# First layer's experts: one written order on TensorE, token transposes around half of the down products, one down tile split

## The chip, the cores and the metric

The kernel runs on one core of one Trainium2 chip. The metric is device time in microseconds of that core, the median of several runs; less is better. Beside the timed runs one execution was recorded by the hardware profiler, and every trace row below comes from that execution.

## The reference, cut to what matters

The program is a two-layer transformer for 1024 latent tokens and 256 context tokens, of width 1024. Each layer ends with 16 experts. An expert takes the 128 latent tokens (and, in the first layer alone, also the 32 context tokens) that score best for it:

```
xg  = h[idx]                                     # 128 x 1024, chosen rows
hid = silu(xg @ w_gate) * (xg @ w_up)            # 128 x 512
out = (hid @ w_down) * vals                      # 128 x 1024
y   = zeros.at[idx].add(out)                     # added back to the tokens
```

The weights of one expert are six tiles of 1 MB: two of `w_gate`, two of `w_up`, two of `w_down`, all in fp32. In the second layer the context tokens are no longer needed (`need` is false there).

## The kernel before, in words

**Products.** `expert_up` computes the gate and up products of the latent tokens as three products of rounded fp32r operands: a weight tile `est` is split by `split` into a high part (`ewh`, a cast on ScalarE, L1178) and a low part (`ewl`, a subtraction on VectorE that reads `est` and `ewh`, L1182), and the tokens into `xh` and `xo`; the products are `xh*wh`, `xo*wh`, `xh*wl` (L1280). The split tiles live in three buffers each. The down products of the latent tokens (`pd`, L1335) are plain fp32 products on the unsplit tile; each is recorded as two passes of TensorE. The context tokens are only 32 rows, so their products run with `tile_position`, four at a time, each in 32 columns of the array: gate and up as `pgc` (L1265), two folding steps as `hcp` (L1309), down as `pdc` (L1341). I call such products quarter products.

**Tokens.** `expert_x` turns the gathered rows: four transposes into PSUM bank 4 (`xt`, L1231), a multiplication on VectorE (`xm`, L1233), an addition on GpSimd (L1234), a cast on ScalarE (`xh`, L1235), a subtraction on VectorE (`xo`, L1236), and the same again for the second four; then two transposes `xtc` for the context tokens, with `xct` on VectorE. `expert_hid` makes `hid`, transposes it through the same bank 4 (`hidp`, L1300) and copies it to `hidT`; it also folds the context part (`hcp`), computes `hidc` and transposes it (`hct`, L1317). `slots` (L1148) finds the tokens of a later expert with ten tiny products `slp`.

**Order.** The program is written as a loop over 16 experts: slots and loads of expert e+3, `expert_hid(e)`, `expert_x(e+2)`, `expert_up(e+1)`, `expert_down(e)`. That is not the order on the engines: a planner runs the program once in its own timing model and places every instruction on its engine's queue when the model finds it ready. On the chip each queue then runs in exactly that order, and waits for data by semaphores. `issue_after` tells the planner to place an instruction behind another.

**Loads.** SyncE issues the weight loads into a ring of nine `est` buffers, in the order gate and up of expert e, then down of expert e-1. GpSimd issues the gathers (`xg`, `xgc`) and the scatters that add an expert's result to the tokens in DRAM (`yo`, `yc`, L1170).

**Banks.** PSUM has eight banks. Gate and up of the latent tokens use banks 0 and 1, down 2 and 3, `xt` and `hidp` share bank 4, `pgc` has bank 5, and `hcp`, `hct` and `pdc` share bank 6.

Of the kernel before, what the change touches and what calls it, by code (L numbers as in the profile page):

```python
# [19 lines left out]
P = 128  # L20
# [22 lines left out]
class Kern:  # L43
# [1177 lines left out]
    def expert_x(self, l, r, ep, eng=None):  # L1221
# [6 lines left out]
        for k in range(0, KD, 4):  # L1228
            ps = self.bank("xt" if need else "xt2", [P, 4, P], F32, "xt")
            for j in range(4):  # L1230
                nc.tensor.transpose(ps[:, j], xg[:, (k + j) * P:(k + j + 1) * P], self.idf)  # L1231
            xm = ep.tile([P, 4, P], F32, name="xm", bufs=2)
            nc.vector.tensor_tensor(xm, ps, self.A2[:, 0, k:k + 4].unsqueeze(2).to_broadcast([P, 4, P]), ALU.mult)  # L1233
            (eng or nc.gpsimd).tensor_tensor(xm, xm, mt[:, 0, 24 + k:28 + k].unsqueeze(2).to_broadcast([P, 4, P]), ALU.add)  # L1234
            nc.scalar.copy(xh[:, k:k + 4], xm)  # L1235
            r["xd"] = nc.vector.tensor_tensor(xo[:, k:k + 4], xm, xh[:, k:k + 4], ALU.subtract)  # L1236
        r["x"] = (xh, xo)
        if need:
# [4 lines left out]
            for c in range(2):  # L1243
                nc.tensor.transpose(ps[:, c], xgc[:, c * P:(c + 1) * P], self.idf)
# [5 lines left out]

    def expert_up(self, l, r, ep, first=False):
# [4 lines left out]
        pc, sc = None, []  # L1256

        def ctx_mm(gu, hf, st):

            nonlocal pc  # L1260
            if hf == 0:
                pc = self.bank("upc", [P, 512], F32, "pgc")
            for k in range(4):
                kk = 4 * hf + k
                nc.tensor.matmul(pc[32 * k:32 * k + 32], r["xc"][:, kk % 2, 32 * (kk // 2):32 * (kk // 2) + 32],  # L1265
                                 st[:, 512 * k:512 * k + 512], start=hf == 0, stop=hf == 1, tile_position=(0, 32 * k),
                                 skip_group_check=True)
            if hf == 1:
                t = ep.tile([P, 512], F32, name=f"sc{gu}", bufs=1)
                nc.scalar.copy(t, pc)  # L1270
                sc.append(t)
        late = []
        for gu in range(2):
            n = 0
            for hf in range(2):
                st = r[("gate", "up")[gu]][hf]
                wh, wl = r["pre"].pop(0) if r.get("pre") else self.split(self.ws, st, [P, 2048], "ew", 3)
# [5 lines left out]
                if need:  # L1283
                    late.append((gu, hf, st))
                    if len(late) > 1 * first:
                        ctx_mm(*late.pop(0))
        for x in late:
            ctx_mm(*x)
        return acc, sc

    def expert_hid(self, l, r, up, ep):
        nc = self.nc
        need = l < DEPTH - 1
        (pg, pu), sc = up
        hid = ep.tile([P, 512], F32, name="hid", bufs=1 + need)
        nc.scalar.activation(hid, pg, AF.Silu)
        nc.vector.tensor_tensor(hid, hid, pu, ALU.mult)
        ps = self.bank("xt" if need else "downc", [P, 4, P], F32, "hidp")
        for j in range(4):
            nc.tensor.transpose(ps[:, j], hid[:, j * P:(j + 1) * P], self.idf)  # L1300
        hT = ep.tile([P, 4, P], F32, name="hidT", bufs=2)
        nc.scalar.copy(hT, ps)  # L1302
        if need:

            ps = self.bank("downc", [P, 256], F32, "hcp")
# [5 lines left out]
            hc, uc = [ep.tile([64, 256], F32, name=n, bufs=1) for n in ("hidc", "upc")]  # L1311
            nc.scalar.activation(hc, ps[:64], AF.Silu)
            nc.vector.tensor_copy(uc, ps[64:])
            nc.vector.tensor_tensor(hc, hc, uc, ALU.mult)
            ps = self.bank("downc", [P, 2, 64], F32, "hct")
            for c in range(2):
                nc.tensor.transpose(ps[:, c], hc[:, P * c:P * c + P], self.idf[:64, :64])  # L1317
            hcT = ep.tile([P, 2, 2, 32], F32, name="hcT", bufs=2)
            nc.vector.tensor_copy(hcT.rearrange("p h c s -> p c h s"), ps.rearrange("p c (h s) -> p c h s", h=2))
        return hT, (hcT if need else None)  # L1320

    def expert_down(self, l, r, hid, ep, g5, g5c, xl, xc):
# [3 lines left out]
        if need:  # L1326
            pd = self.bank("downc", [P, 512], F32, "pdc")
        po = [self.bank("down", [P, 512], F32, "pd") for _ in range(2)]
        for hf in range(2):
            st = r["down"][hf]  # L1330

            for k in range(2):
                for nn in range(2):
                    c = 1024 * k + 512 * nn
                    self.downed = nc.tensor.matmul(po[nn], hT[:, 2 * hf + k], st[:, c:c + 512],  # L1335
                                                   start=hf == 0 and k == 0, stop=hf == 1 and k == 1)
            for k in range(2):
                if need:
                    for nn in range(2):
                        o = 64 * k + 32 * nn  # L1340
                        nc.tensor.matmul(pd[o:o + 32], hcT[:, hf, k], st[:, 1024 * k + 512 * nn:1024 * k + 512 * nn + 512],  # L1341
# [197 lines left out]
```

## Time and profile before

| what | us |
|---|---|
| median of 3 timed runs | 2732.65 (2731.37 to 2734.65) |
| the profiled execution's own time | 2732.13 |
| its span, first to last instruction | 2730.4 |
| experts of the first layer, first gate product to last down product | 1005.7 to 1447.3 |

The span is 1.7 us below the execution's own time; a change inside the span is added to the 2732.13. The experts of the first layer repeat with one period per expert, so that a change there is read from one period and multiplied. A period can be taken between any two equal events of neighbouring experts; here it is the start of the gate's `silu` on ScalarE.

### The profile page before, as it was taken

To read this page: it belongs to the slowest core of one execution; us is meant where nothing else is said; L and a number is where in the kernel's file an instruction comes from. 1 tells how busy PE (TensorE), PEld (TensorE's weight loads), DVE (VectorE), ACT (ScalarE), POOL (GpSimd) and SP (SyncE) were. 2 spreads that over 40 slices of the span, in tenths; PEclk is the share of its full clock that TensorE was granted. 3 is DMA by queue.
4 is the path that set the end of the run, shared out by engine and by line. 5 is a ranking of instruction groups with operands and counts; after the bars stand their busy time and mean duration, and the time that the engine had idled before them with its cause. 6 is when DMAs were issued, how large, how long until landed. Compare 5 with 4: busy or idle time off the path is not lost.

```text
span 2730.4 us, 55190 instructions
## 1 busy us (share of the span) xinstructions
PE 2504.4 (92%) x21959; PEld 1906.9 (70%) x21959; DVE 1884.3 (69%) x4046; ACT 1131.4 (41%) x1878; POOL 669.3 (25%) x621
## 2 busy tenths in 40 slices
PE   7999999998999979999996999999958899589997
PEld 4998887894677855555554988778844677367664
DVE  4258887857666586777754368787858874787874
ACT  4224433324554534444434334333314554345452
POOL 1000000035444633333311000000045532222241
PEclk9999999998999979999998999999979999789999
DMA  7332324247354948888887332423176355889994
GB/s 281 102 108 71 114 68 123 66 138 243 113 160 135 349 151 278 281 280 279 283 280 212 94 105 74 124 84 89 49 200 225 94 163 183 300 281 370 377 376 127
DMA packets 347936, 507.12 MB, mean 186 GB/s; under 512 B 53380, under 2 KB 203072, under 8 KB 346592
## 3 DMA queue, kind: packets, MB, share of 16 engines
q1 hardware_dynamic: 336416, 465.85, 50.4%
q0 software_dynamic: 11264, 37.75, 5.9%
q8 instruction: 173, 2.83, 0.4%
q14 instruction: 83, 0.68, 0.1%
HBM read 410.10 MB, written 94.90 MB: 185 GB/s over the span
## 4 chain that ended last, share of the span: by engine, by line
PE 67%; DVE 18%; DMA 5%; issue 4%; ACT 3%; POOL 2%; SPq 1%; POOLq 0%; DVEq 0%; ACTq 0%
PE pg L1280 13%; PE pj L277 12%; PE pd L1335 8%; PE pj L288 8%; PE po L828 6%; PE nao L786 3%; PE pgc L1265 2%; PE npt L762 2%; PE sA L733 1%; DVE Kt L375 1%; PE aps L157 1%; DVE Kt L376 1%; DVE Qt L378 1%; PE hl L365 1%; PE xt L1231 1%
## 5 line engine op out<-in xcount | busy, mean ns | idle before, releaser
L1182 DVE TENSOR_TENSOR ewl<-est,ewh 128x2048 fp32r<-128x2048 f32 x126 | 298.1, 2371 | 109.7 <-ACT ewh L1178 108.6
L1178 ACT CAST ewh<-est 128x2048 fp32r<-128x2048 f32 x128 | 243.4, 1905 | 170.9 <-PE pg L1280 130.5
L277 PE MATMUL pj<-hl,whi 128*128 128x320 f32 (+2 forms) x912 | 310.2, 340 | 0.0
L277 PE MATMUL pj<-hh,whi 128*128 128x320 f32 (+2 forms) x912 | 309.9, 340 | 0.0
L277 PE MATMUL pj<-hh,wlo 128*128 128x320 f32 (+2 forms) x912 | 308.7, 339 | 0.0
L288 PE MATMUL pj<-whi,hh 128*128 128x256 f32 x960 | 277.8, 290 | 4.5 <-ACT nev L566 4.1
L288 PE MATMUL pj<-whi,hl 128*128 128x256 f32 x960 | 276.8, 291 | 0.8 <-DVE hl L239 0.8
L288 PE MATMUL pj<-wlo,hh 128*128 128x256 f32 x960 | 275.5, 288 | 0.0
L1335 PE MATMUL pd<-est,hidT 128*128 128x512 f32 x512 | 232.2, 596 | 2.1 <-ACT hidT L1302 2.1
L288 PEld LDWEIGHTS pj<-whi,hh 128*128 128x128 f32 x960 | 186.0, 194 | 8.8 <-ACT nev L566 5.2
L288 PEld LDWEIGHTS pj<-wlo,hh 128*128 128x128 f32 x960 | 185.9, 194 | 2.2 <-issue 1.3
L288 PEld LDWEIGHTS pj<-whi,hl 128*128 128x128 f32 x960 | 184.6, 194 | 3.5 <-issue 1.3
L277 PEld LDWEIGHTS pj<-hh,whi 128*128 128x128 f32 x912 | 172.2, 189 | 13.7 <-issue 0.9
L277 PEld LDWEIGHTS pj<-hl,whi 128*128 128x128 f32 x912 | 172.2, 189 | 13.5 <-issue 1.9
L277 PEld LDWEIGHTS pj<-hh,wlo 128*128 128x128 f32 x912 | 172.1, 189 | 13.0 <-issue 1.1
L1335 PEld LDWEIGHTS pd<-est,hidT 128*128 128x128 f32 x512 | 95.2, 189 | 110.7 <-issue 103.3
L265 DVE TENSOR_TENSOR wlo<-wst,whi 128x1024 fp32r<-128x1024 f32 (+1 forms) x72 | 75.2, 1058 | 131.7 <-ACT whi L264 130.6
L1280 PE MATMUL pg<-ewh,xh 128*128 128x512 f32 x512 | 156.8, 424 | 3.1 <-ACT xh L1235 3.0
L752 POOL TENSOR_SCALAR S<-S,sm 128x768 f32<-128x768 f32 (+2 forms) x108 | 108.6, 1007 | 188.3 <-DVE sm L751 166.8
L1280 PE MATMUL pg<-ewl,xh 128*128 128x512 f32 x512 | 147.7, 404 | 0.0
L1280 PE MATMUL pg<-ewh,xo 128*128 128x512 f32 x512 | 142.3, 398 | 2.1 <-DVE xo L1236 2.1
L750 ACT ACTIVATE S<-S,mn 128x768 f32<-128x768 f32 (+2 forms) x108 | 98.6, 913 | 85.2 <-DVE mn L745 79.6
(369 smaller groups left out, 5560.9 us busy)
## 6 DMA issues: line engine op xcount, KB each, us to landing
est<-in_w_exp_gate_dram SPq DMA_DIRECT2D x64, 1024.0 KB
est<-in_w_exp_up_dram SPq DMA_DIRECT2D x64, 1024.0 KB
est<-in_w_exp_down_dram SPq DMA_DIRECT2D x64, 1024.0 KB
wm<-in_w_mod_dram SPq DMA_DIRECT2D x80, 512.0 KB
wst<-in_w_in_dram SPq DMA_DIRECT2D x88, 256.0 KB
pna<-nev SPq DMA_DIRECT2D x180, 64.0 KB
wos<-in_w_out_dram SPq DMA_DIRECT2D x42, 256.0 KB
mst<-mix SPq DMA_DIRECT2D x32, 320.0 KB
```

Of the source, the lines that this page charges most:

```text
L265: nc.vector.tensor_tensor(b, c, a, ALU.subtract)
L277: nc.tensor.matmul(ps[:, :cn], sel(a(k)), b[:, k, c0:c0 + cn], start=n == 0, stop=n == 3 * KD - 1)
L288: nc.tensor.matmul(ps[:, :2 * P], b[:, k, t * P:(t + 1) * P], a(k).rearrange("p a n -> p (a n)"), start=n == 0, stop=n == 3 * KD - 1)
L750: nc.scalar.activation(S[:, :w], S[:, :w], AF.Exp, scale=-1.0, bias=mn[:, 1:2], accum_out=sm[:, 0:1])
L752: nc.gpsimd.tensor_scalar(S[:, :w], S[:, :w], sm[:, 1:2], 1.0, ALU.mult, ALU.mult)
L762: nc.tensor.transpose(pt[:kn, i], S[:, c:c + kn], self.idf)
L786: nc.tensor.matmul(po[64 * X:64 * X + 64, gi], V[:kn, tt, 64 * X:64 * X + 64], PT[X][:kn, i], start=i == 0, stop=i == len(ch) - 1, tile_po ...
L828: nc.tensor.matmul(ps, a, b, start=n == 0, stop=n == len(ops) - 1)
L1178: nc.scalar.copy(hi, src)
L1182: nc.vector.tensor_tensor(lo[:, :m], src[:, :m], hi[:, :m], ALU.subtract)
L1280: nc.tensor.matmul(acc[gu], a[:, 4 * hf + k], b[:, 512 * k:512 * k + 512], start=n == 0, stop=n == 3 * KD - 1)
L1335: self.downed = nc.tensor.matmul(po[nn], hT[:, 2 * hf + k], st[:, c:c + 512], start=hf == 0 and k == 0, stop=hf == 1 and k == 1)
```

## The change

Only the first layer's experts change in what is computed where (the second layer takes the same functions with `need` false; there `hid` of an expert is written behind the down products of the one before, instead of ahead of the next loads).

1. A helper `then` chains every matmul and transpose issued under it behind the one before. TensorE's order becomes the program's: gate products of e+1, all 32 quarter products of gate and up, up products, the fold `hcp`, then the quarter products of down of e, four token transposes of e+2, the first half of down, four more transposes and `xtc`, the second half of down, `hidp` and `hct` of e+1. Only `slp` stays free.
2. The quarter products are no longer interleaved with the split products: `pgc` of gate and up follow each other, in banks 5 and 6, and `hcp`, `hct` move to bank 5.
3. The second of the two down tiles is split (`ewh`, `ewl`), and so is half of `hidT` (`hTh`, `hTl`); that half of down becomes twelve fp32r products instead of four fp32 products (eight passes).
4. `hidc` and its transposes span 128 partitions instead of 64.

```diff
+    def expert_xs(self, l, r, ep, eng=None, order=False):
...
             for j in range(4):
-                nc.tensor.transpose(ps[:, j], xg[:, (k + j) * P:(k + j + 1) * P], self.idf)
+                with self.then(order):
+                    nc.tensor.transpose(ps[:, j], xg[:, (k + j) * P:(k + j + 1) * P], self.idf)
...
+            if k == 0:
+                yield
...
+    @contextmanager
+    def then(self, on=True):
+        nc, tc = self.nc, self.tc
...
+        def after(f):
+            def g(*a, **k):
+                with tc.issue_after(self.pel.ins) if self.pel is not None else nullcontext():
+                    self.pel = f(*a, **k)
+                return self.pel
+            return g
+        nc.tensor.matmul, nc.tensor.transpose = after(mm), after(tr)
...
+        def ctx_mm(gu):
+            pc = self.bank(("upc", "downc")[gu], [P, 512], F32, "pgc")
+            for hf in range(2):
...
+        with self.then(need):
+            prods(0)
+            if need and not first:
+                ctx_mm(0)
+                ctx_mm(1)
+            prods(1)
+            if need and first:
+                ctx_mm(0)
+                ctx_mm(1)
...
+    def expert_ctx(self, sc):
+        ps = self.bank("upc", [P, 256], F32, "hcp")
+        with self.then():
...
+    def expert_ctx_hid(self, ps, ep):
+        hc, uc = ep.tile([P, 256], F32, name="hidc", bufs=1), ep.tile([64, 256], F32, name="upc", bufs=1)
+        nc.scalar.activation(hc, ps, AF.Silu)
+        nc.vector.tensor_copy(uc, ps[64:])
+        nc.vector.tensor_tensor(hc[:64], hc[:64], uc, ALU.mult)
+        pt = self.bank("upc", [P, 2, P], F32, "hct")
+        with self.then():
             for c in range(2):
-                nc.tensor.transpose(ps[:, c], hc[:, P * c:P * c + P], self.idf[:64, :64])
+                nc.tensor.transpose(pt[:, c], hc[:, P * c:P * c + P], self.idf)
...
+            hh, hl = [ep.tile([P, 2, P], F32R, name=n, bufs=2) for n in ("hTh", "hTl")]
+            nc.scalar.copy(hh, hT[:, 2:])
+            nc.vector.tensor_tensor(hl, hT[:, 2:], hh, ALU.subtract)
+            self.hTs = (hh, hl)
...
+    def expert_down(self, l, r, hid, ep, g5, g5c, xl, xc, mid=None):
         if need:
+            hTh, hTl = self.hTs
+            wh, wl = self.split(self.ws, r["down"][1], [P, 2048], "ew", 3)
             pd = self.bank("downc", [P, 512], F32, "pdc")
+            with self.then():
...
+            next(mid, None)
         po = [self.bank("down", [P, 512], F32, "pd") for _ in range(2)]
         for hf in range(2):
+            if hf == 1:
+                next(mid, None)
+            with self.then(need):
...
+                        if need and hf == 1:
+                            for i, (a, b) in enumerate(((hTh, wh), (hTl, wh), (hTh, wl))):
+                                self.downed = nc.tensor.matmul(po[nn], a[:, k], b[:, c:c + 512], start=False,
+                                                               stop=k == 1 and i == 2)
+                            continue
...
             for e in range(NE):
                 if e + 3 <= NE:
                     start(e + 3, rs[e + 1]["xd"])
-                hid = self.expert_hid(l, rs[e], up, ep)
-                if e + 2 < NE:
+                if not need and e + 2 < NE:
                     self.expert_x(l, rs[e + 2], self.xp)
                 if e + 1 < NE:
                     up = self.expert_up(l, rs[e + 1], ep)
-                self.expert_down(l, rs[e], hid, ep, g5, g5c, xl, xc)
+                    if need:
+                        pc = self.expert_ctx(up[1])
+                more = iter(())
+                if need and e + 2 < NE:
+                    more = self.expert_xs(l, rs[e + 2], self.xp, order=True)
+                self.expert_down(l, rs[e], (hid, hidc if need else None), ep, g5, g5c, xl, xc, more)
+                if e + 1 < NE:
+                    hid = self.expert_hid(l, rs[e + 1], up, ep)
+                    if need:
+                        hidc = self.expert_ctx_hid(pc, ep)
```

## Rows read from the trace of the kernel before

**Rows 1.** The page's part 1: busy us, share of the span, instructions
```profile
PE 2504.4 (92%) x21959; PEld 1906.9 (70%) x21959; DVE 1884.3 (69%) x4046; ACT 1131.4 (41%) x1878; POOL 669.3 (25%) x621
```

**Rows 2.** Windows: ten experts' periods; us, engines' busy, granted clock, DMA share, GB/s
```profile
1093.52:1120.77 27.25, 27.25 (x147) 14.84 (x148) 20.74 (x27) 11.87 (x13) 9.15 (x6) 1.00 0.86 283
...
sum 272.32, PE 272.32 PEld 148.49 DVE 203.28 ACT 117.39 POOL 91.53; mean PE 27.23 PEld 14.85 DVE 20.33 ACT 11.74 POOL 9.15
```

**Rows 3.** Waits in these ten experts: total us, times, longest
```profile
DVE ewl L1182 <- ACT ewh L1178: 50.7, 16, 3.7
...
PEld pd L1335 <- issue: 37.1, 130, 0.8
...
ACT ewh L1178 <- DMA est<-in_w_exp_gate_dram: 16.3, 4, 4.4
```

**Rows 4.** Timeline of one period, TensorE: start us, us, instruction
```profile
1220.21 1.07 PE L1280 MATMUL pg<-ewh,xo 128*128 128x512 f32 x4
1221.12 1.07 PE L1280 MATMUL pg<-ewl,xh 128*128 128x512 f32 x4
1222.12 1.06 PE L1265 MATMUL pgc<-est,xct 128*32 128x512 f32 x8
1223.11 0.96 PE L1280 MATMUL pg<-ewh,xh 128*128 128x512 f32 x3
1224.01 1.92 PE L1341 MATMUL pdc<-est,hcT 128*32 128x512 f32 x16
1225.86 0.20 PE L1148 MATMUL slp<-pay,O 128*128 128x5 bf16 x2
1225.93 0.64 PE L1231 MATMUL xt<-idf,xg 128*128 128x128 f32 x4
1226.32 0.48 PE L1280 MATMUL pg<-ewh,xh 128*128 128x512 f32 x1
...
1228.55 1.07 PE L1265 MATMUL pgc<-est,xct 128*32 128x512 f32 x8
...
1232.15 0.64 PE L1309 MATMUL hcp<-sc,sel 128*32 128x256 f32 x8
...
1240.94 1.92 PE L1265 MATMUL pgc<-est,xct 128*32 128x512 f32 x16
1242.80 2.84 PE L1335 MATMUL pd<-est,hidT 128*128 128x512 f32 x6
```

**Rows 5.** Timeline, TensorE's weight loads of two neighbouring passes of down
```profile
1243.33 0.19 PEld L1335 LDWEIGHTS pd<-est,hidT 128*128 128x128 f32 x1 [0.24 <-issue]
1243.76 0.19 PEld L1335 LDWEIGHTS pd<-est,hidT 128*128 128x128 f32 x1 [0.24 <-issue]
```

**Rows 6.** Groups by line, the ten experts: busy us, mean ns, idle before
```profile
L1182 DVE TENSOR_TENSOR ewl<-est,ewh 128x2048 fp32r<-128x2048 f32 x40 | 94.6, 2365 | 50.7 <-ACT ewh L1178 50.7
L1178 ACT CAST ewh<-est 128x2048 fp32r<-128x2048 f32 x40 | 76.2, 1905 | 51.2 <-PE pg L1280 31.9 <-DMA est<-in_w_exp_gate_dram 16.3 <-DVE xm L1233 3.0
...
L1234 POOL TENSOR_TENSOR xm<-xm,mt 128x512 f32<-128x512 f32 x20 | 20.9, 1046 | 3.4 <-DVE xm L1233 3.2
...
L1233 DVE TENSOR_TENSOR xm<-xt,A 128x512 f32<-128x512 f32 x20 | 13.8, 692 | 2.8 <-PE hcp L1309 1.6 <-PE xt L1231 0.3 <-issue 0.2
L1236 DVE TENSOR_TENSOR xo<-xm,xh 128x512 fp32r<-128x512 f32 x20 | 13.6, 681 | 0.0
L1235 ACT CAST xh<-xm 128x512 fp32r<-128x512 f32 x20 | 12.3, 615 | 2.6 <-POOL xm L1234 2.6
...
L1248 DVE TENSOR_TENSOR xct<-xct,mt 128x256 f32<-128x256 f32 x10 | 4.2, 417 | 0.0
```

**Rows 7.** GpSimd's scatter of the context result, from 1093.52 us on: ns min/median/max
```profile
L1170 POOL DMA_INDIRECT c<-yc,ixd x15: 1417/3483/3495, 1093.9 to 1461.1; - x15
```

**Rows 8.** Timeline: TensorE's waits at the first and the last expert
```profile
1024.12 2.13 PE L1280 MATMUL pg<-ewh,xh 128*128 128x512 f32 x8 [0.97 <-ACT xh L1235]
...
1440.27 7.13 PE L1335 MATMUL pd<-est,hidT 128*128 128x512 f32 x16 [0.73 <-ACT hidT L1302]
```

More of the change, by code (lines that the diff above doesn't have):

```diff
@@ L1 @@
-from contextlib import ExitStack, nullcontext
+from contextlib import ExitStack, contextmanager, nullcontext
 import math
@@ L1219, in expert_w, with expert_x @@
                 r[n].append(st)
-    def expert_x(self, l, r, ep, eng=None):
+    def expert_x(self, *a, **k):
+        for _ in self.expert_xs(*a, **k):
+            pass
+    def expert_xs(self, l, r, ep, eng=None, order=False):
         nc = self.nc
@@ L1242, in expert_x @@
             ps = self.bank("small", [P, 2, P], F32, "xtc")
-            for c in range(2):
-                nc.tensor.transpose(ps[:, c], xgc[:, c * P:(c + 1) * P], self.idf)
+            with self.then(order):
+                for c in range(2):
+                    nc.tensor.transpose(ps[:, c], xgc[:, c * P:(c + 1) * P], self.idf)
             v = lambda t: t.rearrange("p c (i s) -> p c i s", i=4)
@@ L1249, in expert_x @@
             r["xc"] = xc
+    @contextmanager
+    def then(self, on=True):
+        nc, tc = self.nc, self.tc
+        if not on:
+            yield
+            return
+        mm, tr = nc.tensor.matmul, nc.tensor.transpose
+        def after(f):
[5 more added lines that the diff above has]
+        nc.tensor.matmul, nc.tensor.transpose = after(mm), after(tr)
+        try:
+            yield
+        finally:
+            nc.tensor.matmul, nc.tensor.transpose = mm, tr
     def expert_up(self, l, r, ep, first=False):
@@ L1255, in expert_up, with prods @@
         acc = [self.bank("up", [P, 512], F32, "pg") for _ in range(2)]
[L1256 to L1273, printed above, removed]
+        sc = []
+        def prods(gu):
             n = 0
             for hf in range(2):
-                st = r[("gate", "up")[gu]][hf]
-                wh, wl = r["pre"].pop(0) if r.get("pre") else self.split(self.ws, st, [P, 2048], "ew", 3)
+                wh, wl = r["pre"].pop(0) if r.get("pre") else self.split(self.ws, r[("gate", "up")[gu]][hf], [P, 2048],
+                                                                         "ew", 3)
                 for a, b in ((xh, wh), (xo, wh), (xh, wl)):
@@ new lines, in expert_hid @@
+    def expert_hid(self, l, r, up, ep):
+        nc = self.nc
+        need = l < DEPTH - 1
+        (pg, pu), _ = up
+        hid = ep.tile([P, 512], F32, name="hid", bufs=1 + need)
+        nc.scalar.activation(hid, pg, AF.Silu)
+        nc.vector.tensor_tensor(hid, hid, pu, ALU.mult)
+        ps = self.bank("xt" if need else "downc", [P, 4, P], F32, "hidp")
+        with self.then(need):
+            for j in range(4):
+                nc.tensor.transpose(ps[:, j], hid[:, j * P:(j + 1) * P], self.idf)
+        hT = ep.tile([P, 4, P], F32, name="hidT", bufs=2)
+        nc.scalar.copy(hT, ps)
+        if need:
[3 more added lines that the diff above has]
+            self.hTs = (hh, hl)
+        return hT
```

72 lines of the change are left out of this document (33 added, 39 removed).

## The prediction, on record before the run

> **What bounds the kernel now.** I read the page's part 1 first: TensorE is busy for 92% of the span, far ahead of VectorE with 69% [rows 1]. A share over the whole span proves little, so the second view was the busy time by windows, one window to an expert of the first layer. Ten neighbouring periods have TensorE busy throughout, 27.23 us of 27.23, at a granted clock of 1.00 (the 2.4 GHz level), while VectorE works 20.33, ScalarE 11.74 and GpSimd 9.15 us [rows 2]. The DMA share of 0.86 is high but its rate of 283 GB/s is not constant over a period, and nothing on TensorE waits for it. The third view, the waits, says that too: what TensorE's weight loads waited for is "issue", that is, the pass in front [rows 3]. ScalarE does wait for late gate tiles, 16.3 us in ten experts, without TensorE feeling it. So this stage is bound by the sum of what TensorE streams, and the change is priced from the spacing of its instructions. The timeline gives that spacing.
>
> **TensorE's prices.** I take the distance between starts, not the durations, since neighbouring matmuls overlap. Four fp32r products of 512 columns take 0.91 us from group to group [rows 4], 0.2275 each. A pass of an fp32 product takes 0.43 [rows 5], so one fp32 product costs 0.86. Eight quarter products together: a group of 16 takes 1.86 to the next start and a group of 8 takes 0.99 [rows 4], so eight more cost 0.87. But a group also costs something on going in and out. The product group ahead of `pgc` takes 1.00 instead of 0.91, `pgc` 0.99 instead of 0.87, and the first product behind it has about 0.1 more: the three following take 0.90 to the next quarter group, of which again 0.09 are the way in, against 0.68 for three. That is 0.09 + 0.12 + 0.13, about 0.34 us for each change of the array's form and back.
>
> The whole period checks it: 48 fp32r products 10.92; 16 passes of down 6.88; 48 quarter products (32 `pgc`, 16 `pdc`) six times 0.87, 5.22; `hcp` with half the columns 0.43; 16 transposes at 0.1 (four take 0.39 [rows 4]) 1.6; ten `slp` 0.3. That sums to 25.35, and 27.23 - 25.35 = 1.88 remain for five groups (`pgc`, `pdc`, `pgc`, `hcp`, `pgc` in rows 4), 0.38 each. I use 0.35.
>
> **The change part by part.**
>
> *Fixed order, quarter products together.* After it there are two groups in a period: 32 `pgc`, and `hcp` with `pdc` straight behind. Three changes of form fall away: 3 x 0.35 = 1.05 us per expert. Bounds: 3 x 0.30 and 3 x 0.38, 0.9 to 1.15. `hct` over 128 partitions costs at most two hundredths more and removes another odd form; I count nothing.
>
> *Half of down split.* Eight passes, 8 x 0.43 = 3.44, become twelve fp32r products, 12 x 0.2275 = 2.73: 0.71 less per expert. It adds to ScalarE a cast of 1.905 us and a copy of 128x256 (between 0.3 and 0.6, from `xh` of twice the size), and to VectorE a subtraction of 2.365 and one of 128x256, 0.42 [rows 6]. ScalarE goes to about 14.1 us of a period, no matter. VectorE goes from 20.33 to 23.1. The split tile is wanted 3/4 into the period; its buffer is free after the gate products, so the split itself has over 10 us of cover.
>
> *Loads.* A `down` tile is now released when half of down is done, earlier than now, where `pdc` comes only in the next expert's gate products; `pgc` releases the gate and up tiles in the first 10 us of a period. SyncE's queue stands in the same order, and its waits for ring buffers end earlier. I cost this at nothing; the cover is the nine-tile ring. Were it gone, the late gate tiles of today, 16.3 us in ten experts [rows 3], would reach TensorE with 1.6 us each.
>
> *Second layer.* It has the same instructions; only `hid` is written a little earlier in the program. No row prices that; I count nothing, with a wait like those of rows 8, up to 1 us, as a bound on either side.
>
> *The sum.* 1.05 + 0.71 = 1.76 per expert, a period of 25.47. Fifteen turns of the loop hold the full saving and the last expert only the split: 15 x 1.76 + 0.71 = 27.1 us.
>
> *What the fixed order costs.* The planner can no longer put other work in front of a late operand. Three places:
>
> (a) Start. The first expert's `hcp` and `hct` now stand ahead of the second expert's gate products, and each waits for a short chain of ScalarE and VectorE work. Waits for such a chain today are 0.97 and 0.73 us [rows 8]. Two of them: 2 us; bounds 0 and 5 (VectorE is behind in that stretch).
>
> (b) Bank 4. It is handed on twice within the down products: `xt` first half, then second half, then `hidp`. VectorE must have read the bank (0.692) before the next may write. Between the first two handovers lie eight passes, 3.44 us; between the second two, two transposes and twelve products, 2.95 us. If one subtraction of 2.365 is in front, VectorE is done after 3.06: no wait at the first, 0.1 to 0.3 at the second. Behind a transpose that waits, the whole rest of the order is queued: the second half of down, `hidp`, the next gate products; and `yo`, with its scatter, is late by as much.
>
> (c) Tokens. The transposed tokens of e+2 are made just ahead of their use. From the last `xt` to the first gate product that reads its half lie `xtc`, half of down, `hidp`, `hct`, `slp` and twelve products: 0.2 + 2.73 + 0.6 + 0.3 + 2.73 = 6.6 us. The chain is transpose 0.3, VectorE 0.69, GpSimd 1.05, ScalarE 0.62 [rows 6]: 2.7. Four us of slack.
>
> Unknown is the order that the planner gives VectorE, which will be busy 23.1 of 25.5 us, 91%. For (b) and (c) together I take 0.4 us per expert, 6 us in all; lower bound nothing, upper bound in the rivals.
>
> Total: 27.1 - 2 - 6 = 19 us less. 2732.1 - 19 = 2713. The medians stand 0.5 us above the profiled execution, within their spread.
>
> **The rivals.**
>
> *Transposed tokens late through GpSimd: no change.* The context scatter occupies GpSimd for 3.483 us in a typical expert and only 1.417 at best [rows 7]. If it stands in front of the second `xm` addition, the chain of (c) is 2.7 + 3.5 = 6.2, and with one subtraction on VectorE ahead of it 8.5, against 6.6 to be had: TensorE waits 1.9 us, 15 times, 28 us, and the gain is gone: 2732. Against it: the scatter must wait for `yc`, which the new order makes earlier, and the addition itself never took more than about 1.05 in the steady stretch. The Trainium skill, GPSIMD Engine Reference, section 8 (Key points), says that GpSimd shares its SBUF interfaces with VectorE and contends with VectorE instructions that have two SBUF inputs. The change adds just such instructions, five large subtractions per expert instead of four, so by that rule the scatters get longer; the trace agrees as far as the scatter's 3.483 against 1.417 goes, and not for the addition.
>
> *VectorE's order at bank 4: slower.* If two subtractions stand in front of `xm`, VectorE needs 5.4 us: a wait of 2.0 at the first handover, 2.5 at the second. At one of the two: 30 to 37 us for 15 experts against 25.1 (27.1 less the start), 2737 to 2744. At both: 67 us, 2774. It decides from 1.7 us of waiting per expert. For it: 91% of an engine with strict order, whose idle time today (6.9 us of a period, of which 5.1 wait for `ewh` [rows 3]) shows that it does stand waiting in front of work that is ready. Against it: each `ewl` has 5 us and more before its product is due, so the planner has room to put `xm` first.
>
> *It only half does it.* `slp` stays free. If it lands within a quarter group, it splits that group: 0.35 each, up to two per expert, 10 us back: 2723. Waits of 0.8 instead of 0.4 give about the same, 2719.
>
> *No waits at all.* 2732.1 - 27.1 = 2705, or 2707 with the start.
>
> **How the numbers follow.** Forecast with small waits, 2705 to 2720: 0.54. Half of it, 2720 to 2727: 0.14. Tokens late or an equal loss, 2727 to 2738: 0.14. VectorE's order, above 2738: 0.18, half of it below 2745. What a measurement can tell from no change is 0.2%, 5.5 us; so faster 0.68, same 0.14, slower 0.18. The range from 2704 to 2745 leaves out about 0.1 above and a few hundredths below; the likeliest case alone has 2705 to 2720.
>
> **What would show it.** A period near 25.5 to 25.9 by windows, with VectorE about 23 us of it; two quarter groups of 32 and 24 in TensorE's timeline, 12 fp32r products in the second half of down at 0.23 spacing. Wrong would be waits of TensorE for `xm` ahead of `xt` or `hidp` (bank 4), for `xh` or `xo` ahead of the gate products, or for `ewl`; a period over 27; or a second layer whose experts take longer than before.

## The result and the profile after

The changed kernel takes 2704.5 us, median of four runs (2703.19 to 2707.69), beside 2733.65 us for the kernel before on the same chip: a ratio of 0.9896 [0.9884, 0.9909], by which it is 28.4 us less. The forecast was 2713 with a range from 2704 to 2745. The profiled execution took 2707.69 us with a span of 2706.0; it is the slowest of the four, and its first gate product comes 3.45 us later than in the profile of before (1009.12 against 1005.67), ahead of all that was changed. I therefore count from the first gate product. One run of experiment 2 took 3148.79 us at a lower granted clock, and its figures leave that run out.

Busy time over the span, which answers to [rows 1], says little again: TensorE still has 92%.

```profile
PE 2484.9 (92%) x22023; PEld 1932.9 (71%) x22023; DVE 1924.3 (71%) x4078; ACT 1167.6 (43%) x1910; POOL 664.5 (25%) x621
```

Ten periods by windows (us, then the engines' busy time, granted clock, DMA share, GB/s), the answer to [rows 2]:

```profile
1122.04:1147.58 25.54, 25.54 (x154) 16.09 (x150) 22.79 (x29) 14.08 (x16) 9.20 (x6) 1.00 0.89 300
...
sum 255.31, PE 255.31 PEld 160.70 DVE 227.60 ACT 140.91 POOL 91.98; mean PE 25.53 PEld 16.07 DVE 22.76 ACT 14.09 POOL 9.20
```

A period is 25.53 instead of 27.23, forecast 25.47; TensorE is still never idle in it. VectorE has 22.76 (forecast 23.1), ScalarE 14.09 (forecast 14.1). The waits of the same stretch, beside [rows 3]: the longest are off TensorE, and its own weight loads wait for "issue" alone.

```profile
ACT xh L1240 <- POOL xm L1239: 61.7, 20, 3.3
...
PEld pgc L1271 <- issue: 18.6, 62, 0.4
```

One period in TensorE's timeline (start, us, instruction), beside [rows 4]:

```profile
1197.85 3.64 PE L1271 MATMUL pgc<-est,xct 128*32 128x512 f32 x32
1201.42 1.19 PE L1271 MATMUL pg<-ewh,xh 128*128 128x512 f32 x4
...
1207.24 0.64 PE L1271 MATMUL hcp<-sc,sel 128*32 128x256 f32 x8
1207.69 1.90 PE L1271 MATMUL pdc<-est,hcT 128*32 128x512 f32 x16
1209.52 0.66 PE L1271 MATMUL xt<-idf,xg 128*128 128x128 f32 x4
1210.02 3.60 PE L1271 MATMUL pd<-est,hidT 128*128 128x512 f32 x8
1213.45 0.60 PE L1271 MATMUL xt<-idf,xg 128*128 128x128 f32 x4
...
1214.03 0.48 PE L1271 MATMUL pd<-ewh,hTh 128*128 128x512 f32 x1
...
1216.87 0.60 PE L1271 MATMUL hidp<-idf,hid 128*128 128x128 f32 x4
```

Two groups of quarter products stand where five stood. The 32 `pgc` take 3.57 us from start to start, and the twelve products of the split half of down 2.84 (1214.03 to 1216.87), 0.23 each.

The forecast's two worries meet in the same stretch on VectorE and GpSimd (timeline of those engines):

```profile
1208.38 2.29 DVE L1182 TENSOR_TENSOR ewl<-est,ewh 128x2048 fp32r<-128x2048 f32 x1
...
1211.16 0.69 DVE L1238 TENSOR_TENSOR xm<-xt,A 128x512 f32<-128x512 f32 x1
...
1214.26 1.67 POOL L1170 DMA_INDIRECT c<-yc,ixd  x1 [1.22 <-DVE yc L1412]
...
1214.51 0.67 DVE L1238 TENSOR_TENSOR xm<-xt,A 128x512 f32<-128x512 f32 x1
...
1215.44 1.56 POOL L1239 TENSOR_TENSOR xm<-xm,mt 128x512 f32<-128x512 f32 x1
1215.55 1.75 DVE L1256 TENSOR_TENSOR xct<-xct,mt 128x256 f32<-128x256 f32 x1
```

One subtraction of 2.29 stands in front of `xm`, as term (b) supposed. VectorE has read bank 4 at 1211.85, and the next transposes come at 1213.45: 1.6 us to spare. And the context scatter does stand ahead of the second `xm` addition, as the rival of late tokens supposed, but takes 1.67 us. Groups by line over the ten experts (busy us, mean ns, idle before), beside [rows 6, 7], show how such times shifted (the 1298 ns of `xm` is the mean of some 1.03 us for the first half and 1.56 for the second):

```profile
L1165 POOL DMA_INDIRECT xg<-h2l,ix x10 | 28.6, 2860 | 37.5 <-DVE val L1160 37.5
L1239 POOL TENSOR_TENSOR xm<-xm,mt 128x512 f32<-128x512 f32 x20 | 26.0, 1298 | 61.0 <-DVE xm L1238 61.0
L1256 DVE TENSOR_TENSOR xct<-xct,mt 128x256 f32<-128x256 f32 x10 | 17.5, 1747 | 0.3
L1170 POOL DMA_INDIRECT c<-yc,ixd x10 | 16.7, 1667 | 12.2 <-DVE yc L1412 12.2
```

**Where the time went,** by events of both traces, counted from the first gate product:

| stretch | before | after | difference |
|---|---|---|---|
| first gate product to the third expert's `silu` | 60.36 | 61.88 | +1.52 |
| eleven periods, third to fourteenth `silu` | 299.81 | 280.80 | -19.01 |
| fourteenth to sixteenth `silu` | 54.29 | 50.65 | -3.64 |
| last `silu` to last down product | 26.69 | 26.00 | -0.69 |
| last down product to the second layer's first transposes | 28.52 | 13.74 | -14.78 |
| from there to the second layer's first gate product | 925.82 | 934.50 | +8.68 |
| the rest (second layer's experts) | 329.25 | 329.30 | +0.05 |

Together 27.9 us less. Two rows were not in the forecast: the end of the stage, and what the second layer's stretch behind it took more.

**The start.** TensorE's timeline ahead of the second expert's gate products, beside [rows 8]:

```profile
1031.34 0.63 PE L1271 MATMUL hcp<-sc,sel 128*32 128x256 f32 x4
1033.78 0.92 PE L1271 MATMUL hcp<-sc,sel 128*32 128x256 f32 x4 [1.81 <-ACT sc L1309]
...
1036.45 0.38 PE L1148 MATMUL slp<-pay,O 128*128 128x5 bf16 x8 [1.60 <-DVE val L1160]
1037.20 0.66 PE L1271 MATMUL hct<-idf,hidc 128*128 128x128 f32 x2 [0.37 <-DVE ixd L1156]
1037.51 2.06 PE L1271 MATMUL pg<-ewh,xh 128*128 128x512 f32 x4
```

The window behind the waits (columns as in the windows above):

```profile
1037.50:1041.00 3.50, 3.50 (x11) 2.78 (x10) 0.29 (x1) 0.00 (x0) 1.89 (x2) 0.53 1.05 415
```

Three waits, 3.78 us, and behind them a granted clock of 0.53, near the lower of the two levels (1.2 GHz): two groups of four take 3.45 us to the next start instead of 1.82.

**The end.** TensorE and GpSimd in the timeline of before, around the last context products:

```profile
1455.89 1.90 PE L1341 MATMUL pdc<-est,hcT 128*32 128x512 f32 x16
...
1461.07 1.43 POOL L1170 DMA_INDIRECT c<-yc,ixd  x1 [10.49 <-DVE yc L1352]
...
1475.33 1.09 PE L234 MATMUL ps<-idf,x 128*128 128x128 f32 x4 [16.24 <-DVE rs1x L203]
```

The same in the timeline of after:

```profile
1420.52 1.92 PE L1271 MATMUL pdc<-est,hcT 128*32 128x512 f32 x16 [0.43 <-ACT hidT L1361]
...
1424.86 1.42 POOL L1170 DMA_INDIRECT c<-yc,ixd  x1 [2.79 <-DVE yc L1412]
...
1442.19 1.11 PE L234 MATMUL ps<-idf,x 128*128 128x128 f32 x4 [4.82 <-DVE rs1x L203]
```

Before, the last down products ended at 1447.4, and the last expert's context part ran behind them, among the next layer's modulation products `aps` (not shown). Its scatter was issued at 1461.07, and the load of the context tokens in front of the second layer waited for it; the chain of before says so:

```profile
1461.07 3.77 DMA c<-yc,ixd
...
1466.43 5.90 DMA x<-c
...
1478.99 1.20 PE pj L288 x4
```

After, the program has the last context part ahead of the last down products; its scatter is issued 3.6 us before the last of these. What the second layer's first projections `pj` wait for is then their weights, in the chain of after:

```profile
1441.49 6.08 DMA wst<-in_w_in_dram
...
1447.80 0.94 ACT whi L264
1448.78 0.80 PE pj L288 x2
```

The first `pj` comes 6.59 us behind the first transposes, 3.66 before the change (1478.99 in the chain above, against 1475.33): 2.9 us of the 14.78 are given back at once.

### The profile page after: what moved, and what is told of

Same layout as the page of the kernel before. It is cut to its first block, busy times and chain, and to the rows that moved or that the text cites. A ratio compares the mean times of both kernels' runs of the same rounds, so it can differ in the third digit from the quotient of the medians.

```text
span 2706.0 us, 55370 instructions
## 1 busy us (share of the span) xinstructions
PE 2484.9 (92%) x22023; PEld 1932.9 (71%) x22023; DVE 1924.3 (71%) x4078; ACT 1167.6 (43%) x1910; POOL 664.5 (25%) x621
## 4 chain that ended last, share of the span: by engine, by line
PE 67%; DVE 16%; DMA 7%; issue 3%; ACT 3%; POOL 2%; SPq 1%; POOLq 0%; DVEq 0%; ACTq 0%
PE pj L277 13%; PE pj L288 8%; PE pg L1271 7%; PE pg L1294 6%; PE po L828 5%; PE pd L1401 4%; PE pd L1271 4%; PE nao L786 3%; PE npt L762 2%; PE pgc L1271 2%; PE aps L157 2%; PE sA L733 1%; PE hl L341 1%; DVE Kt L375 1%; PE hl L365 1%
## 5 line engine op out<-in xcount | busy, mean ns | idle before, releaser
L1182 DVE TENSOR_TENSOR ewl<-est,ewh 128x2048 fp32r<-128x2048 f32 x142 | 331.0, 2336 | 70.6 <-ACT ewh L1178 69.8
L1178 ACT CAST ewh<-est 128x2048 fp32r<-128x2048 f32 x144 | 273.7, 1906 | 134.8 <-PE pg L1294 85.5
L1239 POOL TENSOR_TENSOR xm<-xm,mt 128x512 f32<-128x512 f32 x60 | 82.7, 1389 | 160.4 <-DVE xm L1238 142.1
L157 PE MATMUL aps<-wm,sT 128*32 128x512 f32 x320 | 84.5, 673 | 40.1 <-POOL E L639 28.4
L786 PE MATMUL nao<-PT,nav 128*64 128x128 f32 (+1 forms) x1296 | 113.8, 282 | 6.0 <-ACT PT L765 4.6
L354 ACT COPY kz<-Kt 64x320 f32<-64x320 f32 x120 | 54.9, 466 | 147.2 <-DVE Kt L375 119.0
L509 POOL TENSOR_TENSOR hos<-hos,hrs 128x512 f32<-128x512 f32 (+1 forms) x15 | 19.7, 1312 | 396.6 <-DVE hrs L508 361.0
```

Source lines behind the costliest of these rows:

```text
L157: nc.tensor.matmul(ps[32 * j:32 * j + 32], self.sT[:, k, :], w[j], start=k == 0, stop=k == KD - 1, tile_position=(0, 32 * j))
L786: nc.tensor.matmul(po[64 * X:64 * X + 64, gi], V[:kn, tt, 64 * X:64 * X + 64], PT[X][:kn, i], start=i == 0, stop=i == len(ch) - 1, tile_po ...
L1178: nc.scalar.copy(hi, src)
L1182: nc.vector.tensor_tensor(lo[:, :m], src[:, :m], hi[:, :m], ALU.subtract)
```

## The experiments

Each is the changed kernel with one edit, unless it says otherwise. Ratios are to the kernel before on the same chip; periods are from `silu` to `silu` in the steady stretch.

**1. The second down tile not split.**

```diff
-            wh, wl = self.split(self.ws, r["down"][1], [P, 2048], "ew", 3)
...
-                        if need and hf == 1:
-                            for i, (a, b) in enumerate(((hTh, wh), (hTl, wh), (hTh, wl))):
```

> Fixed order kept, but the second down tile is not split: its half of down is four fp32 products (eight passes) again. Theory 1 (the stage is the sum of what TensorE streams): eight passes at 0.43 us instead of twelve products at 0.2275, so the period goes from 25.53 to 26.24 us, the time from 2704.5 to 2716, and VectorE's busy time in a period falls from 22.8 to about 20.1. Rival (the order alone made the gain, the split is hidden): period 25.5, time 2704. Rival (VectorE at 89% holds TensorE up somewhere): with 2.7 us less on VectorE the period stays below 26.1.

2719.72 us, 0.9959 [0.9942, 0.9976]; period 26.19, so the split is worth 0.66 here; 0.71 was the price.

**2. The context products of gate and up in four groups again,** between the split products.

```diff
-            prods(0)
-            if need and not first:
-                ctx_mm(0)
-                ctx_mm(1)
-            prods(1)
+            on = need and not first
+            prods(0, {12: lambda: ctx_mm(0, (0,)), 24: lambda: ctx_mm(0, (1,))} if on else None)
+            prods(1, {4: lambda: ctx_mm(1, (0,)), 12: lambda: ctx_mm(1, (1,))} if on else None)
```

> TensorE's order is fixed as in the changed kernel, but the 32 quarter products of gate and up are spread over four groups of eight (after each half of gate, after a third of the first half of up, after the first half of up): five groups in a period instead of two, the same products. Theory 1 (each change of the array's form and back costs about 0.35 us): 3 x 0.35 = 1.05 more, period 26.6, time 2720. Rival (it is the fixed order that gains, not the number of groups): period 25.5, time 2704.

2738.27 us, 1.0024 [1.0014, 1.0034]; period 27.87. TensorE's timeline:

```profile
1203.42 1.07 PE L1271 MATMUL pgc<-est,xct 128*32 128x512 f32 x8 [0.28 <-DVE hcT L1350]
...
1209.50 1.06 PE L1271 MATMUL pgc<-est,xct 128*32 128x512 f32 x6
1210.49 0.20 PE L1148 MATMUL slp<-pay,O 128*128 128x5 bf16 x2
1210.63 1.05 PE L1271 MATMUL pgc<-est,xct 128*32 128x512 f32 x2
1211.61 1.20 PE L1271 MATMUL pg<-ewh,xo 128*128 128x512 f32 x4
```

Three more whole groups at the forecast's 0.34 would cost 1.02. But here two `slp` broke up a group: its eight take 2.11 us from start to start instead of 0.99, 1.12 more. With the wait of 0.28 that is 2.42, against 27.87 - 25.53 = 2.34 measured, so that 0.94 is left for the three groups, 0.31 each. The two leftover `pgc` alone take 0.98, as long as eight: four quarter products (two passes each) run side by side, and a set that is cut takes its full time twice. The forecast had 0.35 for an `slp` in a group.

**3. Five groups, and the slot products chained** behind the last quarter group of the gate (the edit beside experiment 2).

```diff
+            if slots:
+                slots()
             prods(1, {4: lambda: ctx_mm(1, (0,)), 12: lambda: ctx_mm(1, (1,))} if on else None)
```

> The run with the context products in five groups took 27.87 us per period, and 1.1 us of it stood where the planner had put two of the free slot products inside a quarter group. Here the five groups stay and the ten slot products are chained too, behind the last quarter group of the gate, so that none can stand inside a group. Theory 1 (the slot products inside a group cost 1.1 us and nothing else differs): a period of 26.6 to 26.8, 2719 to 2724 in all. Rival (the five groups themselves cost more than three times 0.35, and the slot products only stand where the time would be lost anyway): a period of 27.5 to 27.9, 2733 to 2739.

2784.35 us, 1.0197 [1.0181, 1.0212]; period about 31.0. Neither came: chaining them made a wait. TensorE's timeline:

```profile
1202.14 0.20 PE L1271 MATMUL slp<-pay,O 128*128 128x5 bf16 x2 [2.28 <-DVE val L1160]
...
1205.17 1.87 PE L1271 MATMUL pg<-ewh,xo 128*128 128x512 f32 x4
```

The window behind the wait:

```profile
1203.30:1206.90 3.60, 3.60 (x14) 1.59 (x14) 0.00 (x0) 0.00 (x0) 0.98 (x1) 0.54 1.01 388
```

The ten `slp` write one bank in two lots, and the second lot waits until VectorE has reduced the first; with the order written out, all of TensorE waits with it. The granted clock behind the wait is 0.54: the quarter group takes 1.86 and the next four 1.71 us, 1.7 more than at full clock. Less 2.28, another wait of 0.47 for `hcT`, and 1.7, 31.0 comes to 26.55: 1.02 above the changed kernel, three groups at 0.34. The 1.7 is a difference of spacings, so that this is an estimate.

**4. Both halves of the token transposes together** ahead of the down products.

```diff
             next(mid, None)
+            next(mid, None)
...
-            if hf == 1:
-                next(mid, None)
```

> Changed kernel, but the second four token transposes stand right behind the first four, ahead of all down products, so that nothing lies between the two uses of bank 4. Theory 1 (the down products between them hide VectorE's read of the bank): TensorE now waits for the transposes' end and VectorE's 0.68 us, some 0.9 us per expert where VectorE is free at once, up to 3.2 where a subtraction is in front: period 26.4 to 27, time 2717 to 2727. Rival (the place does not matter, the planner shifts VectorE's work): 25.5, 2704.

2753.11 us, 1.0082 [1.0065, 1.0099], slower than before the change; periods of 28.6 and 30.2. TensorE and VectorE in the timeline of that run:

```profile
1200.19 2.28 DVE L1182 TENSOR_TENSOR ewl<-est,ewh 128x2048 fp32r<-128x2048 f32 x1
...
1202.96 0.69 DVE L1238 TENSOR_TENSOR xm<-xt,A 128x512 f32<-128x512 f32 x1
...
1203.71 1.05 PE L1271 MATMUL xt<-idf,xg 128*128 128x128 f32 x4 [1.79 <-DVE xm L1238]
...
1204.99 4.72 PE L1271 MATMUL pd<-est,hidT 128*128 128x512 f32 x8
```

This is term (b) with its cover taken away: the same single subtraction in front of `xm`, and now 1.79 us of wait. The granted clock over 1203.70 to 1209.00 is 0.68, and the eight passes of down take 4.15 to the next start instead of 3.43. So the eight passes between the handovers are what hides VectorE. Of the 3.0 us more in the shorter periods the wait is 1.79; a `pgc` group that `slp` cuts into 18 and 14 takes 4.68 instead of 3.57, 1.11 more. The longer periods, 4.7 us more, have the lowered clock besides; in a shorter one the same stretch, 1292.70 to 1298.00, stands at 1.00.

**5. Only the split, on the kernel before** (planner's order kept).

```diff
+            wh, wl = self.split(self.ws, r["down"][1], [P, 2048], "ew", 3)
...
+                    if need and hf == 1:
+                        for i, (a, b) in enumerate(((hTh, wh), (hTl, wh), (hTh, wl))):
```

> The kernel before with one part of the change alone: the second down tile split, its half of down as twelve fp32r products; order, banks and loop as before. Theory 1 (the parts add up on TensorE): period 27.23 - 0.71 = 26.5, the end of the stage as before, time 2722. Rival (the split needs the fixed order, since the planner runs into VectorE): period 27 and more, time 2728 or more.

2738.28 us, 1.0032 [1.0017, 1.0047]; periods alternate, mostly between 26.5 to 27 and 28 to 28.5. The parts do not add: with the planner's order the split gains nothing. One reason shows in the timeline, that the planner then cuts quarter sets: in one period a `pgc` group of eight stands as two and six with `hct` in between, 0.97 and 0.99 us long.

**6. All of the change but the written order** (`then` does nothing).

```diff
-        if not on:
+        if True:
             yield
             return
```

> Everything of the changed kernel, but the helper that chains TensorE's instructions does nothing, so that the planner orders TensorE itself, from the same program order and with the split down tile. Theory 1 (the fixed order gains by keeping the quarter products in two groups): the planner breaks the groups up again, five or more in a period as before, period 26.4 to 27.5, time 2712 to 2735. Rival (the program order and the banks already give it, the chain adds nothing): period 25.5, time 2704.

2722.62 us, 0.9969 [0.9957, 0.998]; period 26.94, again with cut sets (`pdc` as 6 and 10 around two `slp`) and an uneven start with turns from 16.0 to 32.9. The written order is worth 26.94 - 25.53 = 1.41 per period. Most of it is that cut set: the 16 `pdc` take 2.93 us to the next start instead of 1.83, 1.10 more, and there is one quarter group more. At the end of the stage the first transposes of the second layer come 13.93 us behind the last down product, as early as with the written order; in experiment 5, with the loop of before, 26.67.

**7. The last expert's context products late again,** behind its latent down products.

```diff
+        if need and late:
+            pd = quarters(hcT())
...
-                        hidc = self.expert_ctx_hid(pc, ep)
+                        hidc = self.expert_ctx_hid(pc, ep) if e + 2 < NE else lambda: self.expert_ctx_hid(pc, ep)
```

> Changed kernel, but the last expert's context products (the transposes of its hidden part and the quarter products of down) stand behind its latent down products, next to the modulation products of the second layer, as in the kernel before. Theory (some 6 to 11 us of the gain lie behind the last down product, since the second layer's first loads wait for the last scatter of context rows): the last context scatter is issued 8 to 11 us later than at 1424.9, the second layer's first transposes start 6 to 11 us later, time 2710 to 2716; the periods stay 25.53. Rival (that difference comes from elsewhere or is scatter between runs): time 2702 to 2707.

2715.93 us, 0.9942 [0.9924, 0.9961], periods unchanged. The last context scatter moves to 1436.54, 9.2 us behind the last down product, and the second layer's first transposes come 19.27 us behind it instead of 13.74. The whole is some 11 to 13 us longer than the changed kernel. The trace shows 5.5 of them at this place; the rest lies behind, in a stretch that differs by as much between profiles without such an edit, and is not shown to come from it.

**8. The written order dropped ahead of the loop,** for the first expert.

```diff
-        if not on:
+        if not on or self.free:
...
+            self.free = True
...
+            self.free = False
             for e in range(NE):
```

> The changed kernel with the written order dropped for the first expert's gate and up products, fold and transposes ahead of the loop; the loop keeps it. The first turn took 23.25 us against 19.46 before the change. Theory 1 (the written order costs the start about 3 to 4 us, by waits for short chains of ScalarE and VectorE): the first two turns together 44 to 45.5 instead of 48.4, 2700 to 2702 in all. Rival (the first turn is long because TensorE's clock is down there and the split tiles come late, whatever the order): the first two turns 47.5 to 49, 2704 to 2706.

2705.31 us, 0.9904 [0.989, 0.9919], no different from the change. The first two turns take 47.65 instead of 48.37 (44.9 before the change): the rival was right that this order is not the cause. The planner's order ahead of the loop waits too, 3.03 us at `slp` for `val`, and the granted clock behind it is 0.50 over 1043.50 to 1047.00.

**9. Both down tiles split.** The split hidden part, now twice as large, has one buffer instead of two, here and in experiments 10 to 12.

```diff
-            wh, wl = self.split(self.ws, r["down"][1], [P, 2048], "ew", 3)
+            ws = [self.split(self.ws, r["down"][hf], [P, 2048], "ew", 3) for hf in range(2)]
```

> Both down tiles split, so that all of down runs as fp32r products. Theory 1 (TensorE's sum alone): another 0.71 us less, period 24.8, time 2693. Rival (VectorE): it gets one more subtraction of 2.28 us and 0.3 for the second half of the hidden part, 22.8 + 2.6 = 25.4 us, more than TensorE's 24.8; the period is then at least 25.4, in strict order with waits 25.6 to 26.5, and the time 2704 to 2720, with TensorE waiting for xm or ewl.

2722.2 us, 0.9967 [0.9955, 0.998]; periods mostly 25.45, some 24.5 and 27.2. VectorE is busy 236.51 of 254.60 us, 93%, and TensorE waits for it:

```profile
PEld pg L1271 <- DVE xo L1241: 9.2, 10, 1.6
```

**10. Both split, and the tokens' scaling on ScalarE** (`xm` as four activations with scale and bias, in place of VectorE and GpSimd).

```diff
+                    nc.scalar.activation(xm[:, j], ps[:, j], AF.Identity, bias=mt[:, 0, 24 + k + j:25 + k + j],
+                                         scale=self.A2[:, 0, k + j:k + j + 1])
```

> Both down tiles split, and the tokens' multiplication (VectorE, 2 x 0.68 us) and addition (GpSimd, 2 x 1.3 us) replaced by ScalarE activations with scale and bias straight from PSUM, eight of 128 columns per expert. Theory 1 (with both tiles split VectorE is what holds the period at 25.45, and ScalarE has 11 us free): VectorE falls to about 24.0 us, TensorE's sum of 24.8 decides again, period 24.8 to 25.1, time 2692 to 2698 against 2704 for the changed kernel. Rival (VectorE at 97% still stands in front, or ScalarE's eight activations delay the casts): period 25.4 or more, time 2704 or more.

2714.69 us, 0.9947 [0.993, 0.9963]; period 26.0: 0.68 a wait for `xo`, and 0.42 a `pgc` group of 32 cut as 24 and 8 (3.99 us with its `slp`, instead of 3.57). A cut between whole sets of eight costs about one change of form; one inside a set cost 1.12 (experiment 2).

**11. As 10, with the slot products chained and the second half of the gate taking `xo` last.**

```diff
-                for a, b in ((xh, wh), (xo, wh), (xh, wl)):
+                for a, b in ((xh, wh), (xh, wl), (xo, wh)) if need and gu == 0 and hf == 1 else ((xh, wh), (xo, wh), (xh, wl)):
```

> Both down tiles split and the tokens' scaling on ScalarE took 26.0 us per period: 0.69 of it a wait for the second half of the tokens' low part, 0.4 a quarter group broken up by slot products. Here the ten slot products are chained behind the quarter group, and the second half of the gate takes its products in another order, the low part last. Theory (each is a stall of its own and goes): a period of 24.8 to 25.0, 2692 to 2698 in all, faster than the changed kernel's 2704.5. Rival (VectorE sets the pace of a period with both tiles split, and the wait comes back at another operand): a period of 25.4 to 26.0 with a wait of TensorE for a low part or a split weight, 2704 to 2715.

2734.7 us, 1.0015 [1.0003, 1.0028]; periods alternate 26.46 and 28.08. Neither theory: the wait for `xo` is gone, and it is the bank of `slp` again, at 1.56 us in each expert. In every second one the clock falls behind it, in TensorE's timeline:

```profile
1238.52 0.20 PE L1277 MATMUL slp<-pay,O 128*128 128x5 bf16 x2 [1.56 <-DVE val L1160]
...
1240.01 1.91 PE L1277 MATMUL pg<-ewh,xo 128*128 128x512 f32 x4
```

And in the window behind the wait:

```profile
1238.50:1243.00 4.50, 4.48 (x14) 3.54 (x15) 0.42 (x4) 1.04 (x1) 1.98 (x2) 0.62 1.03 396
```

**12. As 11, the two lots of slot products apart:** eight behind the quarter group, two behind the up products (the edit beside experiment 11).

```diff
             if slots:
-                slots()
+                slots((0,))
             prods(1)
+            if slots:
+                slots((1,))
```

> As the run with both down tiles split and the slot products chained, but the eight slot products of the latent tokens and the two of the context tokens no longer stand together: the eight stay behind the quarter group, the two are chained behind the up products, 5.5 us later. In that run TensorE waited 1.56 us in each expert at the second of the two for VectorE's reduction of the first, since both write one bank, and every second period was 1.6 us longer again, with products of four at 1.4 to 1.9 us instead of 0.91 behind the wait. Theory (wait and lowered clock are one cause, and nothing else is in the way): periods of 24.8 to 25.0, 2691 to 2698 in all, faster than the changed kernel. Rival (VectorE, with both tiles split, comes up next): periods of 25.3 to 26.2 with a wait of TensorE for a low part, 2702 to 2715.

2695.98 us, 0.9886 [0.9867, 0.9905], four runs from 2690.37 to 2700.84; period 24.73, no wait of TensorE in it. Ten periods in one window:

```profile
1102.00:1349.30 247.30, 247.30 (x1544) 167.76 (x1540) 220.61 (x271) 188.28 (x230) 72.29 (x40) 1.00 0.91 308
```

The theory was right: with the lots apart, the wait and the lowered clock are both gone. TensorE is busy throughout at a granted clock of 1.00, VectorE 89%. The period is 0.80 shorter than the changed kernel's, where the split of the other half is worth 0.7. In the traces the stretch from the first gate to the last down product is 411.8 us, against 419.3 after the change and 441.1 before. Of the whole time the runs spread by 10 us. The ratios to the kernel before, 0.9886 and 0.9896, differ by some 3 us and their intervals overlap (the medians differ by 8, but come from two chips): that it beats the changed kernel's total is not shown.

## Why the prediction was right, and where its terms were off

**Bound and prices: right.** The stage is bound by what TensorE streams. Forecast 25.47, measured 25.53, and the parts measured alone agree: three groups 0.94 and 1.02 (experiments 2 and 3; 1.05 forecast), half of down 0.66 (experiment 1; 0.71 forecast). The thirteen steady turns and the last down products give 19.01 + 3.64 + 0.69 = 23.3 us, where 13 x 1.76 + 0.71 = 23.6 was the sum. The Trainium skill, TensorEngine Tiling (Array Packing), Key Properties (under Tiling Modes), says that a change of tiling mode drains TensorE. The 0.31 to 0.34 us per group agrees, and the page gives no figure.

**Terms (b) and (c), 0.4 us per expert: mis-sized; it was nothing.** That is 6 us of the 8.5 between 2713 and 2704.5. The lower bound was the right value. The mechanism is real, though: one subtraction stands in front of `xm`, as supposed, and experiment 4 shows a wait of 1.79 us at the same place when the passes that hide it are moved away. What I had in hand said so already: 3.44 us of cover against 3.06 of VectorE, and I charged the uncertainty as if it were a cost.

**The start, 2 us: mis-sized.** The stretch from the first gate product to the third `silu` holds two turns and should have been 2 x 1.76 = 3.5 us shorter; it is 1.5 longer, so the start costs 5.0, the upper bound. (The two turns alone are 3.5 longer; 2.0 are gained ahead of the first `silu`.) The waits add up to 3.8, and the lowered clock behind them, 1.6 more, was not in the term. Its cause as I gave it, the written order, fell with experiment 8: dropped ahead of the loop, the same stretch loses as much by another wait. In both, part of the wait is that of a lot of `slp` until VectorE has reduced the lot before it (`val`); why the new program runs into it there and the one before does not is open.

**The end of the stage, nothing: wrong.** I followed the period and the start and did not ask what the second layer's first load waits for. It was the last context scatter, 14 us behind the last down product; the change moves it ahead. That gave 14.8 us at its place. Experiment 7 shows the mechanism by undoing a part of it: with the scatter 9.2 us behind, the transposes come 5.5 later. Experiments 5 and 6 tell what brings it: the loop, which has the last context part ahead of the last down products, and not the written order (13.93 without that order, 26.67 with the loop of before). 8.7 us stand against it later in the second layer. 2.9 of them come at once, where `pj` waits for its weights. The rest is not settled: that stretch took 931.9 to 940.1 us in the experiments' profiles, 934.1 in experiment 5, whose end is late as before, so that the 925.8 in the profile of before is the lowest of all and not shown to be lost by the change.

**Half of it, `slp` inside a group at 0.35: right between sets, wrong inside one.** In the changed kernel no `slp` stands inside a group. Experiments 2 and 10 show 1.12 inside and 0.42 between.

**Tokens late through GpSimd: the order came, the loss did not.** The scatter stands in front of the addition, but at 1.67 us, not 3.48 [rows 7], and `xh` is ready in time. By the Trainium skill, GPSIMD Engine Reference, section 8 (Key points), GpSimd contends with VectorE instructions that have two SBUF inputs. The trace agrees, and in these rows the one that starts second pays: VectorE's addition of `xct`, started 0.11 us behind the GpSimd addition of `xm`, takes 1.75 us (0.417 before), its product for `hidc` beside the other addition 0.948 (0.409 before), and before the change it was `yc`, 1.93 beside an addition and 0.735 now, alone. The additions themselves took 1.03 to 1.07 beside `yc` and `hidc`; of the 1.56 at 1215.44, 0.49 are still the record of the scatter, so that the trace does not show them slowed. What the rule did not tell is who would start behind whom: before, the scatter started just behind an `ewl` subtraction (3.48 us), now the gather does (2.86, 0.995 before), and neither is waited for by TensorE.

**VectorE's order at bank 4: did not happen.** Experiment 4 is its neighbour, not the same case: one subtraction in front, not two, and the cover taken away. It ends above the time before, as the rival had it for waits at this place.

**Loads and the second layer's experts, nothing: right.** ScalarE waited 16.3 us for late gate tiles in ten experts before [rows 3]; after the change its casts wait for TensorE alone, 24.6 us. The second layer's experts take 329.30 us, 329.25 before.

**The sum.** -19 forecast; -6 for waits that did not come, +3.0 at the start, -14.8 at the end, +8.7 given back: -28.1, against -27.9 from the two traces and -28.4 from the ratio. That the total lies within the range, half a us above its lower end, is luck in part: the end of the stage, net -6.1, was in no term, and the start's excess of 3.0 happened to stand against it.

## What to carry to other kernels

Where one engine is busy throughout a stage, price its instructions by the distance of their starts and check the sum against the period; then look at both ends of the stage, and ask what the next stage's first load waits for. When you write an order out, give each handover of a shared buffer other work between it and its use: here the same products in another place made the kernel slower than before. If TensorE waits in such an order, count more than the wait, since the clock behind it fell in several of these runs, and put the lots that share one buffer apart.

## What was not expected of the hardware

- Waits of TensorE of 1.6 to 2.3 us were followed by windows of 3.5 to 5.3 us at a granted clock of 0.53 to 0.68 (the start of the changed kernel, experiments 3, 4 and 11), a further loss of 0.7 to 1.7 us. In experiments 4 and 11 the same wait was followed by it in some periods only; in the others the clock stayed at 1.00.
- A quarter group of two passes takes 0.98 us and one of eight 0.99: four quarter products run side by side, and a group that is cut inside a set of eight passes costs 1.11 to 1.12 us (experiments 2 and 4), between sets 0.42.
- An addition of 128x256 on VectorE with two SBUF inputs took 1.75 us when it started just behind a GpSimd addition, and 0.417 on average in the trace of before. A GpSimd gather that started just behind a subtraction of VectorE took 2.86 us instead of 0.995.
